# Straight operand stores, interleaved reads of PSUM: one change to a fused transformer kernel

## The chip, the cores and the metric

The kernel runs on one core of one Trainium2 chip. TensorE (PE) does the matrix products, VectorE (DVE), ScalarE (ACT) and GpSimd (POOL) the elementwise work, and SyncE (SP) issues the transfers. The metric is the device time of one launch in microseconds, as the median of several runs.

## The reference

One sequence of 512 tokens and 1024 channels goes through two blocks, in fp32. The first has two layers, each a mixer and a convolutional FFN; the second has two layers, each with four parallel branches, a mixture of experts and a per-layer gate.

```python
def first_block(x, ...):                       # DEPTH = 2
    for layer in range(DEPTH):
        n = rmsnorm(h, norm_g)
        h = h + (rglru_mixer(n, ...) if layer % 2 == 0 else nsa_mixer(n, ...))
        h = h + conv_ffn(rmsnorm(h, ffn_norm_g[layer]), ...)
    return rmsnorm(h, final_norm_g)

def rglru_mixer(x, ...):
    y_br, x_br = jnp.split(x @ w_in, 2, axis=-1)
    xc = causal_dwconv(x_br, conv_w, conv_b)           # 4 taps
    g = sigmoid(blockwise(xc @ gate_w) + gate_b)       # 10 blocks of 128, two gates
    ...                                                # a, bterm from the gates
    h = associative_scan(a, bterm)
    return (h * gelu(y_br)) @ w_out

def conv_ffn(x, ...):
    a, b = jnp.split(x @ w_in, 2, axis=-1)
    return (gelu(causal_dwconv(a, conv_w, conv_b)) * b) @ w_out

def second_block(x, p, ...):
    for i in range(DEPTH):
        h = rms_norm(x, g_mix[i])
        branches = [gqa(h), bidir_ssd(h), diff_attention(h), spatial_gating(h)]   # 256 wide each
        gates = sigmoid(h @ w_branch_gate[i])          # 4 x 1024
        x = x + sum_n(gates_n * (branches_n @ w_branch[i, n])) @ w_out[i]
        x = x + expert_choice_moe(rms_norm(x, g_moe[i]), ...)      # 16 experts, 64 tokens each
        x = x + sigmoid(rms_norm(x, g_ple[i]) @ w_ple_gate[i]) * (p[i] @ w_ple[i])
    return rms_norm(x, g_final)
```

## The kernel before

Activations are kept transposed: channels on the 128 partitions, the 512 tokens along the columns, eight tiles of channels in `hT`. Each fp32 operand is held as two fp32r parts, a high one and the rest, so a product takes three matmuls of 512 columns: high by high, low by high, high by low (`dense`, L443 to L445, and `proj_wide`, L453 to L455). Weights come as a stream of chunks of 512 KB, of which ACT makes the high part (`wh`, L237) and DVE, in some stretches POOL, the low part (`wl`, L238).

Activation operands are made the same way: ACT writes the high part, DVE the rest. `split` (L350, L351) does it for finished rows (xch and xcl of the recurrent blocks, uh and ul, gh and gl in the FFN, oh and ol of the branches, bch and bcl of the state-space branch), `feed` (L360, L361) for the normalised input of a projection (xh, xl), and `mixer_out` (L1264, L1265) for the merged branches.

The matmuls always read the operand through `woven`, that is in the address order 0, 256, 1, 257 and so on. What PSUM then holds depends on how the operand was stored. Most operands are stored through `woven` too: the writer goes through the source in address order and jumps by 256 columns (1024 bytes) at each element, so PSUM's columns come out straight and are read straight. The feeds of the NSA input and of the second block's branches, the NSA's compressed rows and a part of the state-space operands are stored straight; PSUM's columns are then interleaved, and their first reader undoes it with `halves(out), unwoven(ps)`, which writes two halves of 256 columns from a PSUM read with a step of two. The RMS norm's factor is applied behind the product, by that reader (times `RB`).

There is no planner: each engine runs its instructions in the order in which the code issues them. In the recurrent mixer `xfront(i)` (projection, four taps, split) is issued ahead of `xback(i - 1)` (two gates, L519 to L523), then come ten `yblock` (L541 to L548) and the output projection. In the second block `gate_merge` (L1206 to L1216) runs between the pieces of the next branch; behind the last branch its rows end in `mu` (L1215), POOL adds them to `mg`, and `mixer_out` turns `mg` into the operand of the output projection.

Of the kernel before, what the change touches and what calls it, by code (L numbers as in the profile page):

```python
# [11 lines left out]
F32 = mybir.dt.float32  # L12
# [3 lines left out]
OP = mybir.AluOpType  # L16
# [3 lines left out]
P = 128  # L20
# [262 lines left out]
class Kern:  # L283
# [174 lines left out]
    def proj(self, name, idx, col, m=P):  # L458
# [5 lines left out]
        return ps  # L464

    def res_out(self, name, idx, uh, ul, rows, after):
        nc = self.nc
        for d in range(KD):
            ps = self.psum()
            self.dense(ps, [(name, idx, r, d * P) for r in rows], uh, ul)  # L470
            nc.vector.tensor_add(self.hT[:, d, :], ps, self.hT[:, d, :])
            if after:
                after(d)

    def rglru(self, nxt):
        nc = self.nc
        with ExitStack() as es:
# [20 lines left out]
            def xfront(i):  # L498
                ps = self.proj("lru_w_in", 0, LRU + i * P)
                x = xp[i % 2]  # L500
                nc.vector.tensor_mul(x[:, 3:3 + S], ps, self.RB)
                c = two.tile([P, S], F32, name="c")
                nc.scalar.activation(c, x[:, 3:3 + S], AF.Identity, scale=self.p("lru_cw", 3 * LB + i),
                                     bias=self.p("lru_cb", i))
                for j in range(3):
                    nc.vector.scalar_tensor_tensor(c, x[:, j:j + S], self.p("lru_cw", j * LB + i), c,
                                                   op0=OP.mult, op1=OP.add)
                xch = two.tile([P, S], F32R, name="xch")
                xcl = two.tile([P, S], F32R, name="xcl")
# [30 lines left out]
            def yblock(i):  # L540
                ps = self.proj("lru_w_in", 0, i * P)  # L541
                y = two.tile([P, S], F32, name="y")
                nc.vector.tensor_mul(y, ps, self.RB)
                nc.scalar.activation(y, y, AF.Gelu_apprx_tanh)
# [45 lines left out]
    def ffn(self, l, nxt, side=iter(())):  # L590
        nc = self.nc
        HB = FB // 2
        with ExitStack() as es:
# [9 lines left out]
            def pair(f):  # L603
                ps = self.proj("ffn_w_in", l, f * P)
                a = ap[f % 2]
                nc.vector.tensor_mul(a[:, 2:2 + S], ps, self.RB)
                c0 = two.tile([P, S], F32, name="fc0")
# [8 lines left out]
                g = two.tile([P, S], F32, name="g")  # L616
                nc.vector.tensor_mul(g, pb, c0)
                GH.append(ring.tile([P, S], F32R, name="gh"))
# [18 lines left out]
    def nsa(self, nxt):  # L637
        nc = self.nc
        W = "nsa_w_in"
        with ExitStack() as es:  # L640
# [17 lines left out]
            for j in range(2):  # L658
# [13 lines left out]
                CL.append(cp.tile([P, CW], F32R, name=f"cfl{j}"))  # L672
                self.split(CH[j], CL[j], cf, False)

# [106 lines left out]
            def oproj(half, ds, after):  # L781
# [5 lines left out]
                for d in ds:  # L787
                    ps = self.psum()
                    self.dense(ps, [("nsa_w_out", 0, (half * 4 + j) * P, d * P) for j in range(4)], uh, ul)
                    nc.vector.tensor_add(self.hT[:, d, :], ps, self.hT[:, d, :])  # L790
                    if after:
                        after(d)
                    yield
# [118 lines left out]
            def finish(qt, g):  # L912
# [12 lines left out]
                qs = slice(qt * P, (qt + 1) * P)  # L925
                hs = slice(qt * P // 2, (qt + 1) * P // 2)
                uh, ul = woven(uh)[:, :, hs], woven(ul)[:, :, hs]
                nc.scalar.activation(uh, plain(u), AF.Copy)
                nc.vector.tensor_sub(ul, plain(u), uh.bitcast(F32))

# [262 lines left out]
    def gate_merge(self, l, n, o, tp, first):  # L1193
        nc = self.nc
        for d in range(KD):
# [15 lines left out]
            if first:  # L1211
                nc.vector.scalar_tensor_tensor(m, t, 1.0, pb, op0=OP.add, op1=OP.mult)
            else:
                u = tp.tile([P, S], F32, name="mu", tag="mg", bufs=3)
                nc.vector.scalar_tensor_tensor(u, t, 1.0, pb, op0=OP.add, op1=OP.mult)  # L1215
                nc.gpsimd.tensor_add(m, m, u)  # L1216
# [42 lines left out]
    def mixer_out(self, l):  # L1259
        nc = self.nc  # L1260
        for d in range(KD):
            m = self.mg[d // 4][:, d % 4]
            xh, xl = woven(self.xh[:, d]), woven(self.xl[:, d])
            nc.scalar.activation(xh, plain(m), AF.Copy, scale=0.5)  # L1264
            nc.vector.scalar_tensor_tensor(xl, plain(m), 0.5, xh.bitcast(F32), op0=OP.mult, op1=OP.subtract)  # L1265
        lg = self.pso.tile([P, S], F32, name="o")
# [10 lines left out]
        for d in range(KD):  # L1277
            ps = self.psum()
            self.dense(ps, [("w_out_2", l, k * P, d * P) for k in range(KD)], self.xh, self.xl)
            h = self.hT[:, d, :]  # L1280
            nc.vector.tensor_add(h, ps, h)
            rr = self.mo2.tile([P, 2, S], F32R, name="rr", tag="xd")
            rh, rl = woven(rr[:, 0]), woven(rr[:, 1])
            nc.scalar.activation(rh, plain(h), AF.Copy, scale=self.p("g_moe", d))
            nc.vector.scalar_tensor_tensor(rl, plain(h), self.p("g_moe", d), rh.bitcast(F32), op0=OP.mult, op1=OP.subtract)
            R[d] = rh, rl
            self.sqlast = self.feed_sq(d, self.sq)
# [25 lines left out]
        self.lg = self.mo2.tile([NE, S], F32, name="lg", tag="sg")  # L1313
        nc.scalar.activation(self.lg, lg[:NE], AF.Copy)
        self.ple_proj(l, 0, pre[0], (1, 2))
# [116 lines left out]
    def gqa_branch(self, l, o, one, two):  # L1432
# [18 lines left out]
        for t in range(T):  # L1451
# [25 lines left out]
            for j, dst in enumerate((QT, KT)):  # L1477
# [6 lines left out]
                if j:  # L1484
                    out, src = woven(dst)[:, :, t * P // 2:(t + 1) * P // 2], plain(src)
                if j:
                    nc.vector.tensor_copy(out, src)
                else:
                    nc.scalar.activation(out, src, AF.Copy)
        E, PE, PO = {}, {}, {}  # L1490

        def logits(qt, h):
# [8 lines left out]
            den = self.small.tile([P, 1], F32, name="gden")  # L1501
            nc.scalar.activation(e, ps, AF.Exp, scale=-1.0, bias=mn, accum_out=den)
            nc.vector.reciprocal(den, den)
            nc.gpsimd.tensor_scalar(e, e, den, 1.0, op0=OP.mult, op1=OP.mult)

        def values(qt, b):
# [8 lines left out]
            if b:  # L1515
                c = slice(qt * P // 2, (qt + 1) * P // 2)
                oh, ol = woven(o[0])[:, :, c], woven(o[1])[:, :, c]
                v = plain(po[:, :256].rearrange("p (b q) -> p b q", b=2))
                nc.scalar.activation(oh, v, AF.Copy)
                nc.vector.tensor_sub(ol, v, oh.bitcast(F32))  # L1520

# [25 lines left out]
    def ssd_branch(self, l, o, one, two):  # L1547
# [52 lines left out]
        def conv(j):  # L1600
# [16 lines left out]
            r = one.tile([P, S], F32R, name=f"bch{j // 2}"), one.tile([P, S], F32R, name=f"bcl{j // 2}")  # L1617
            self.split(*r, c, j >= 4)
            return r
# [17 lines left out]
        for g in range(2):  # L1637
# [5 lines left out]
            for i in range(T):  # L1643
# [4 lines left out]
                nc.tensor.matmul(pg, bl[:, sl], woven(ch), start=False, stop=True)  # L1648
                nc.scalar.activation(G[:, i], pg, AF.Copy)
            yield 0  # L1650
# [213 lines left out]
    def moe(self, l):  # L1864
        nc = self.nc
        keep, two, three = self.mo1, self.mo2, self.mo3
        if True:
# [181 lines left out]
            def combine(pairs, ds, last):  # L2049
                new = [p for p in pairs if p not in DT]  # L2050
                dts = two.tile([P, 2, S], F32R, name="DT", tag="xd") if new else None
                for i, p in enumerate(new):
# [5 lines left out]
                    DT[p] = dts[:, i]  # L2058
                    nc.vector.tensor_scalar(woven(DT[p]), plain(pb), self.c("slot"), None, op0=OP.is_equal)
                for d in ds:  # L2060
                    ps = self.pst.tile([P, S], F32, name="t")
                    for i, p in enumerate(pairs):
# [3 lines left out]
                                         stop=(i == len(pairs) - 1))  # L2066
                    nc.vector.tensor_add(self.hT[:, d, :], ps, self.hT[:, d, :])
                    if last:
# [30 lines left out]
    def ple_proj(self, l, d, ps, part=None):  # L2099
# [4 lines left out]
        if d % 2 == 0:  # L2104
            self.pbs = self.wraw.tile([P, 2, S], F32, name="pbs", tag="wraw")
        nc.scalar.activation(self.pbs[:, d % 2], ps, AF.Copy)
        if d % 2:
            nc.sync.dma_start(self.pbd[:, d - 1:d + 1], self.pbs)

    def ple(self, l):  # L2110
        nc = self.nc
        with ExitStack() as es:
# [5 lines left out]
            for d in range(KD):  # L2118
                pg = self.proj("w_ple_gate_2", l, d * P)
                t = two.tile([P, S], F32, name="pg")  # L2120
                nc.vector.tensor_mul(t, pg, self.RB)
                nc.scalar.activation(t, t, AF.Tanh, scale=0.5)
# [63 lines left out]
```

## Time and profile before

| | |
|---|---|
| median of 3 runs | 3520.5 us (3515.93 to 3523.99) |
| the profiled execution's own time | 3526.27 us |
| its span | 3524.5 us |
| mean granted TensorE clock | 0.981 |
| PE busy | 3373.1 us, 96% of the span, 16172 matmuls |
| DVE busy | 1778.4 us, 50% |
| ACT busy | 1322.8 us, 38% |
| POOL busy | 471.6 us, 13% |

Busy times are sums over one engine; idle time of an engine other than the bottleneck costs nothing by itself. The granted clock is the share of TensorE's full speed that it was given. Times in the rows further down are microseconds from the span's start unless marked ns.

### The profile page before, as it was taken

What the parts mean: (1) busy time and instruction counts of PE and PEld (TensorE: products, weight loads), DVE (VectorE), ACT (ScalarE), POOL (GpSimd) and SP (SyncE); (2) the same over time, 40 slices, a digit from 0 to 9 for tenths busy, and PEclk for the clock granted to TensorE, in tenths of its full rate; (3) what the DMA queues carried; (4) which work ended last, traced back from release to release, by engine and by line L of the source; (5) the groups of instructions that cost most, each with busy time, mean ns of one, the idle gap of its engine ahead of it and who ended that gap; (6) DMA issues with size and microseconds to landing.
All of it is one profiled execution on the core that took longest, in us unless ns stands there. A gap on an engine that the chain in (4) does not pass through costs nothing.

```text
span 3524.5 us, 42265 instructions
## 1 busy us (share of the span) xinstructions
PE 3373.1 (96%) x16172; PEld 2359.2 (67%) x16172; DVE 1778.4 (50%) x3181; ACT 1322.8 (38%) x2211; POOL 471.6 (13%) x354
## 2 busy tenths in 40 slices
PE   6899999999999999999998999999999998999997
PEld 5778888876678888876887433326876887433325
DVE  7755454467766465766666011116666666111016
ACT  5644233356654244445545101004445545100004
POOL 4221011022121012111012000002111012000002
PEclk9999999899999999999999999999999999999998
DMA  3233332210013333212244999995221245999993
GB/s 112 72 102 133 107 102 102 101 54 30 31 60 102 102 102 119 78 66 66 93 174 163 375 404 419 419 419 196 79 72 64 89 179 177 388 404 419 419 419 124
DMA packets 173491, 629.06 MB, mean 178 GB/s; under 512 B 19557, under 2 KB 20069, under 8 KB 172521
## 3 DMA queue, kind: packets, MB, share of 16 engines
q1 hardware_dynamic: 173288, 626.36, 47.3%
q8 instruction: 127, 2.08, 0.2%
q14 instruction: 76, 0.61, 0.1%
HBM read 618.14 MB, written 8.14 MB: 178 GB/s over the span
## 4 chain that ended last, share of the span: by engine, by line
PE 76%; DVE 11%; DMA 5%; ACT 4%; issue 2%; POOL 1%; DVEq 0%; SPq 0%; ACTq 0%; POOLq 0%
PE mm L444 13%; PE mm L443 13%; PE mm L445 13%; PE mm L1987 10%; PE o L1987 5%; DMA eraw<-in_exw 3%; DVE wl L238 2%; PE o L893 1%; DMA wraw<-in_exw 1%; PE t L877 1%; PE mm L1969 1%; PE o L1657 1%; PE o L1796 1%; DMA raw<-in_exw 1%; PE t L1539 1%
## 5 line engine op out<-in xcount | busy, mean ns | idle before, releaser
L443 PE MATMUL mm<-xh,wh 128*128 128x512 f32 (+1 forms) x1936 | 750.8, 388 | 13.4 <-DVE mu L1215 10.7
L445 PE MATMUL mm<-xh,wl 128*128 128x512 f32 (+1 forms) x1936 | 744.4, 385 | 4.3 <-DVE wl L238 3.7
L444 PE MATMUL mm<-xl,wh 128*128 128x512 f32 (+1 forms) x1936 | 744.3, 384 | 0.0
L238 DVE TENSOR_TENSOR wl<-wraw,wh 128x1024 fp32r<-128x1024 f32 x356 | 449.1, 1262 | 302.5 <-ACT wh L237 297.6
L237 ACT ACTIVATE wh<-wraw 128x1024 fp32r<-128x1024 f32 x378 | 398.5, 1055 | 503.5 <-PE mm L444 331.6
L443 PEld LDWEIGHTS mm<-xh,wh 128*128 128x128 f32 (+1 forms) x1936 | 369.0, 191 | 80.0 <-DVE mu L1215 12.6
L445 PEld LDWEIGHTS mm<-xh,wl 128*128 128x128 f32 (+1 forms) x1936 | 368.4, 190 | 65.4 <-issue 5.8
L444 PEld LDWEIGHTS mm<-xl,wh 128*128 128x128 f32 (+1 forms) x1936 | 368.8, 191 | 59.5 <-issue 8.2
L375 POOL TENSOR_TENSOR sq<-sq,sqt 128x512 f32<-128x512 f32 x63 | 101.7, 1615 | 1235.4 <-ACT sqt L372 1228.3
L1987 PE MATMUL mm<-eraw,xe 128*64 128x512 f32 x1024 | 242.7, 599 | 0.4 <-DMA eraw<-in_exw 0.4
L1993 DVE TENSOR_TENSOR hid<-sg,mm 128x512 f32<-128x512 f32 x32 | 22.0, 687 | 362.0 <-PE mm L1987 362.0
L1987 PE MATMUL mm<-raw,xe 128*64 128x512 f32 x656 | 162.0, 599 | 1.3 <-DMA raw<-in_exw 0.9
L1987 PEld LDWEIGHTS mm<-eraw,xe 128*64 128x64 f32 x1024 | 70.9, 137 | 134.6 <-issue 114.1
L614 POOL TENSOR_TENSOR fc<-fc,RB 128x512 f32<-128x512 f32 x48 | 84.4, 1758 | 546.4 <-ACT fc L613 546.4
L443 PE MATMUL mm<-gh,wh 128*128 128x512 f32 x384 | 145.7, 379 | 0.0
L445 PE MATMUL mm<-gh,wl 128*128 128x512 f32 x384 | 145.7, 379 | 0.0
L444 PE MATMUL mm<-gl,wh 128*128 128x512 f32 x384 | 145.6, 379 | 0.0
L1216 POOL TENSOR_TENSOR mg<-mg,mu 128x512 f32<-128x512 f32 x48 | 69.9, 1456 | 565.8 <-DVE mu L1215 520.6
L1987 PE MATMUL o<-eraw,hidT 128*64 128x512 f32 x560 | 137.2, 606 | 4.0 <-DMA eraw<-in_exw 3.1
L2041 ACT ACTIVATE yh<-o,af 128x512 fp32r<-128x512 f32 x32 | 22.0, 687 | 295.6 <-PE o L1987 295.6
L1992 ACT ACTIVATE sg<-mm 128x512 f32<-128x512 f32 x32 | 19.1, 597 | 288.8 <-PE mm L1987 288.6
L2042 DVE SCALAR_TENSOR_TENSOR yl<-o,af,yh 128x512 fp32r<-128x512 f32 x32 | 24.0, 751 | 198.5 <-ACT yh L2041 198.3
(524 smaller groups left out, 5883.0 us busy)
## 6 DMA issues: line engine op xcount, KB each, us to landing
eraw<-in_exw SPq DMA_DIRECT2D x396, 512.0 KB, 9.9
wraw<-in_wst SPq DMA_DIRECT2D x378, 512.0 KB, 3.3
raw<-in_exw SPq DMA_DIRECT2D x234, 512.0 KB, 9.9
wraw<-in_exw SPq DMA_DIRECT2D x136, 512.0 KB, 9.9
pbd<-pbs SPq DMA_DIRECT2D x8, 512.0 KB, 4.8
pb<-pbd SPq DMA_DIRECT2D x4, 1024.0 KB, 11.7
tb<-t5d SPq DMA_DIRECT2D x8, 448.0 KB, 3.3
mixt<-in_mix SPq DMA_DIRECT2D x2, 1344.0 KB, 6.4
```

Source lines behind the costliest of these rows:

```text
L237: kb.nc.scalar.activation(h, raw, AF.Copy)
L238: (kb.nc.gpsimd if self.pool else kb.nc.vector).tensor_sub(l, raw, h.bitcast(F32))
L375: nc.gpsimd.tensor_add(acc, acc, t)
L443: nc.tensor.matmul(out, a, h, start=(k == 0), stop=False)
L444: nc.tensor.matmul(out, a, l, start=False, stop=False)
L445: nc.tensor.matmul(out, b, h, start=False, stop=(k == n - 1))
L614: nc.gpsimd.tensor_mul(c0, c0, self.RB)
L877: nc.tensor.transpose(pt[:, r * P:(r + 1) * P], srcs(i, r), self.ident)
L893: nc.tensor.matmul(o[0][c % 2 * HD:(c % 2 + 1) * HD], lhs(i), pe, start=(c < 2), stop=False)
L1216: nc.gpsimd.tensor_add(m, m, u)
L1539: nc.tensor.transpose(pt[:, kb * P:(kb + 1) * P], e[:, kb * P:(kb + 1) * P], self.ident)
L1987: nc.tensor.matmul(ps[e * CAP:(e + 1) * CAP], x[:, k, off + e * CAP:off + (e + 1) * CAP], raw[:, e], start=(k == 0), stop=(k == KD - 1))
```

## The change

Every operand is stored straight: `split`, `feed`, `mixer_out` and the single writers (attention rows, keys, the router's rows, the experts' scatter matrix) lose `woven` and `plain`. The matmuls and their `woven` read stay. So all PSUM columns now come interleaved, and each first reader that was straight gets `halves` on its output and SBUF inputs and `unwoven` on PSUM. A helper, `add_rows`, does so for the sums into `hT`. The count, order and size of the instructions on each engine stay the same. The diff is cut to one place of each kind:

```diff
-    def split(self, h, l, src, weave=True):
-        if weave:
-            h, l, src = woven(h), woven(l), plain(src)
+    def split(self, h, l, src):
         self.nc.scalar.activation(h, src, AF.Copy)
         self.nc.vector.tensor_sub(l, src, h.bitcast(F32))
 
     def feed(self, k, g, sq=True):
         nc = self.nc
         h = self.hT[:, k, :]
-        xh, xl, x = self.xh[:, k], self.xl[:, k], h
-        if isinstance(g, str) and g not in ("nsa_g", "g_mix", "g_next"):
-            xh, xl, x = woven(xh), woven(xl), plain(h)
+        xh, xl = self.xh[:, k], self.xl[:, k]
         g = self.p(g, k) if isinstance(g, str) else g[:, k:k + 1]
-        nc.scalar.activation(xh, x, AF.Copy, scale=g)
-        nc.vector.scalar_tensor_tensor(xl, x, g, xh.bitcast(F32), op0=OP.mult, op1=OP.subtract)
+        nc.scalar.activation(xh, h, AF.Copy, scale=g)
+        nc.vector.scalar_tensor_tensor(xl, h, g, xh.bitcast(F32), op0=OP.mult, op1=OP.subtract)
...
+    def add_rows(self, d, ps):
+        h = halves(self.hT[:, d])
+        self.nc.vector.tensor_add(h, unwoven(ps), h)
...
             def xfront(i):
-                nc.vector.tensor_mul(x[:, 3:3 + S], ps, self.RB)
+                nc.vector.tensor_mul(halves(x[:, 3:3 + S]), unwoven(ps), halves(self.RB))
...
             def xback(i):
-                    nc.scalar.activation(g, pg, AF.Tanh, scale=0.5, bias=gbh[:, j * LB + i:j * LB + i + 1])
+                    nc.scalar.activation(halves(g), unwoven(pg), AF.Tanh, scale=0.5, bias=gbh[:, j * LB + i:j * LB + i + 1])
...
     def mixer_out(self, l):
-            xh, xl = woven(self.xh[:, d]), woven(self.xl[:, d])
-            nc.scalar.activation(xh, plain(m), AF.Copy, scale=0.5)
-            nc.vector.scalar_tensor_tensor(xl, plain(m), 0.5, xh.bitcast(F32), op0=OP.mult, op1=OP.subtract)
+            xh, xl = self.xh[:, d], self.xl[:, d]
+            nc.scalar.activation(xh, m, AF.Copy, scale=0.5)
+            nc.vector.scalar_tensor_tensor(xl, m, 0.5, xh.bitcast(F32), op0=OP.mult, op1=OP.subtract)
...
-            nc.scalar.activation(e, ps, AF.Exp, scale=-1.0, bias=mn, accum_out=den)
+            nc.scalar.activation(halves(e), unwoven(ps), AF.Exp, scale=-1.0, bias=mn, accum_out=den)
```

The other PSUM readers changed like `xfront`'s are the rows of `yblock`, of the FFN (L606, L617), of `mu` (L1215), of the per-layer gate, and the sums into `hT` of `res_out`, the NSA output, `mixer_out` and the experts. On ACT, like `xback`'s: the softmax of the branch attention (L1502, 32 times), the state-space scores (L1649, 16), the router's logits (L1314, 2) and the per-layer rows (L2106, 16).

## Rows read from the trace of the kernel before

**Rows 1.** The page: busy us (share of the span) and instructions of each engine.

```profile
PE 3373.1 (96%) x16172; PEld 2359.2 (67%) x16172; DVE 1778.4 (50%) x3181; ACT 1322.8 (38%) x2211; POOL 471.6 (13%) x354
```

**Rows 2.** PE's waits, whole span: releaser: us in total, times, longest us.

```profile
PE s L519 <- ACT xch L350: 16.1, 9, 4.0
...
PE mm L443 <- DVE mu L1215: 10.7, 4, 5.1
PE mm L454 <- DVE xl L361: 9.7, 12, 2.3
...
PE s L1646 <- ACT bch L350: 4.4, 4, 1.6
```

**Rows 3.** Windows: us, busy us (instructions) of each engine, granted clock, DMA share, GB/s.

```profile
17.00:28.00 11.00, 5.62 (x23) 3.66 (x22) 11.00 (x9) 5.26 (x7) 9.22 (x5) 1.00 0.29 95
28.00:49.00 21.00, 16.39 (x67) 13.44 (x65) 15.84 (x49) 5.41 (x7) 7.44 (x4) 0.84 0.22 76
49.00:144.00 95.00, 74.79 (x302) 59.12 (x303) 84.09 (x89) 66.83 (x80) 35.23 (x19) 0.95 0.18 61
1022.00:1029.00 7.00, 7.00 (x23) 5.60 (x23) 3.54 (x13) 0.06 (x1) 0.50 (x1) 0.55 0.21 75
1862.00:1869.00 7.00, 6.81 (x18) 5.53 (x19) 2.35 (x3) 1.98 (x3) 2.11 (x1) 0.57 0.69 239
2916.00:2920.00 4.00, 4.00 (x11) 3.24 (x12) 1.70 (x2) 1.21 (x2) 2.05 (x1) 0.58 0.47 157
```

**Rows 4.** Lines, 194 to 243 us: busy us, mean ns | idle before, releasers.

```profile
L360 ACT ACTIVATE xh<-hT,prmt 128x512 fp32r<-128x512 f32 x8 | 9.7, 1212 | 14.7 <-DVE hT L471 12.3 <-DVE ap L601 2.4
...
L361 DVE SCALAR_TENSOR_TENSOR xl<-hT,prmt,xh 128x512 fp32r<-128x512 f32 x8 | 9.4, 1169 | 7.6 <-ACT xh L360 7.6
```

**Rows 5.** Lines, 571 to 628 us.

```profile
L361 DVE SCALAR_TENSOR_TENSOR xl<-hT,prmt,xh 128x512 fp32r<-128x512 f32 x8 | 6.0, 749 | 2.4 <-ACT xh L360 2.4
L360 ACT ACTIVATE xh<-hT,prmt 128x512 fp32r<-128x512 f32 x8 | 5.7, 714 | 9.7 <-DVE hT L471 9.7
```

**Rows 6.** Lines, 1586 to 1588.2 us.

```profile
L351 DVE TENSOR_TENSOR bcl<-cv,bch 128x512 fp32r<-128x512 f32 x1 | 0.7, 680 | 0.0
L350 ACT ACTIVATE bch<-cv 128x512 fp32r<-128x512 f32 x1 | 0.6, 637 | 1.0 <-DVE cv L1616 1.0
```

**Rows 7.** Lines of DVE, whole span.

```profile
L1206 DVE TENSOR_TENSOR mg<-mm,RB 128x512 f32<-128x512 f32 x64 | 44.3, 691 | 33.6 <-PE mm L445 33.5
...
L606 DVE TENSOR_TENSOR ap<-mm,RB 128x512 f32<-128x512 f32 x48 | 33.2, 691 | 21.7 <-PE mm L445 17.7 <-ACT RB L422 4.0
```

**Rows 8.** Lines of ACT, whole span.

```profile
L1502 ACT ACTIVATE e<-s,gmn 128x512 f32<-128x512 f32 x32 | 21.8, 683 | 16.5 <-DVE gmn L1499 14.9 <-DVE gden L1503 1.7
...
L523 ACT ACTIVATE gt<-s,gbh 128x512 f32<-128x512 f32 x20 | 12.8, 679 | 6.4 <-PE s L521 6.3
```

**Rows 9.** PE's waits, 0 to 30 us.

```profile
PE mm L454 <- DVE xl L361: 5.4, 4, 2.3
```

**Rows 10.** Lines of DVE, 8.5 to 28 us.

```profile
L361 DVE SCALAR_TENSOR_TENSOR xl<-hT,prmt,xh 128x512 fp32r<-128x512 f32 x8 | 13.8, 1779 | 0.3 <-ACT xh L360 0.3
```

**Rows 11.** DVE's timeline, 178 to 186 us: start us, us, instruction, idle before.

```profile
178.94 1.12 DVE L351 TENSOR_TENSOR ul<-y,uh 128x512 fp32r<-128x512 f32 x1 [3.25 <-ACT uh L350]
179.91 1.21 DVE L238 TENSOR_TENSOR wl<-wraw,wh 128x1024 fp32r<-128x1024 f32 x1
...
184.94 1.10 DVE L351 TENSOR_TENSOR ul<-y,uh 128x512 fp32r<-128x512 f32 x1 [3.23 <-ACT uh L350]
```

**Rows 12.** ACT's timeline, 177 to 181 us.

```profile
177.79 1.12 ACT L350 ACTIVATE uh<-y 128x512 fp32r<-128x512 f32 x1 [1.38 <-POOL y L545]
178.71 1.05 ACT L237 ACTIVATE wh<-wraw 128x1024 fp32r<-128x1024 f32 x1
```

**Rows 13.** DVE's timeline, 1851 to 1862.5 us.

```profile
1854.86 4.29 DVE L1265 SCALAR_TENSOR_TENSOR xl<-mg,xh 128x512 fp32r<-128x512 f32 x4
...
1861.15 0.99 DVE L1215 SCALAR_TENSOR_TENSOR mu<-mg,mm 128x512 f32<-128x512 f32 x1
```

More of the change, by code (lines that the diff above doesn't have):

```diff
@@ L470, in res_out @@
             self.dense(ps, [(name, idx, r, d * P) for r in rows], uh, ul)
-            nc.vector.tensor_add(self.hT[:, d, :], ps, self.hT[:, d, :])
+            self.add_rows(d, ps)
             if after:
@@ L542, in yblock @@
                 y = two.tile([P, S], F32, name="y")
-                nc.vector.tensor_mul(y, ps, self.RB)
+                nc.vector.tensor_mul(halves(y), unwoven(ps), halves(self.RB))
                 nc.scalar.activation(y, y, AF.Gelu_apprx_tanh)
@@ L605, in pair @@
                 a = ap[f % 2]
-                nc.vector.tensor_mul(a[:, 2:2 + S], ps, self.RB)
+                nc.vector.tensor_mul(halves(a[:, 2:2 + S]), unwoven(ps), halves(self.RB))
                 c0 = two.tile([P, S], F32, name="fc0")
@@ L616, in pair @@
                 g = two.tile([P, S], F32, name="g")
-                nc.vector.tensor_mul(g, pb, c0)
+                nc.vector.tensor_mul(halves(g), unwoven(pb), halves(c0))
                 GH.append(ring.tile([P, S], F32R, name="gh"))
@@ L672, in nsa @@
                 CL.append(cp.tile([P, CW], F32R, name=f"cfl{j}"))
-                self.split(CH[j], CL[j], cf, False)
+                self.split(CH[j], CL[j], cf)
             pv = [self.mm.tile([P, S], F32, name="mm") for _ in range(2)] + \
@@ L789, in oproj @@
                     self.dense(ps, [("nsa_w_out", 0, (half * 4 + j) * P, d * P) for j in range(4)], uh, ul)
-                    nc.vector.tensor_add(self.hT[:, d, :], ps, self.hT[:, d, :])
+                    self.add_rows(d, ps)
                     if after:
@@ L925, in finish @@
                 qs = slice(qt * P, (qt + 1) * P)
[L926 to L929, printed above, removed]
+                self.split(uh[:, :, qs], ul[:, :, qs], u)
             def spread(a, b):
@@ L1211, in gate_merge @@
             if first:
-                nc.vector.scalar_tensor_tensor(m, t, 1.0, pb, op0=OP.add, op1=OP.mult)
+                nc.vector.scalar_tensor_tensor(halves(m), halves(t), 1.0, unwoven(pb), op0=OP.add, op1=OP.mult)
             else:
                 u = tp.tile([P, S], F32, name="mu", tag="mg", bufs=3)
-                nc.vector.scalar_tensor_tensor(u, t, 1.0, pb, op0=OP.add, op1=OP.mult)
+                nc.vector.scalar_tensor_tensor(halves(u), halves(t), 1.0, unwoven(pb), op0=OP.add, op1=OP.mult)
                 nc.gpsimd.tensor_add(m, m, u)
@@ L1280, in mixer_out @@
             h = self.hT[:, d, :]
-            nc.vector.tensor_add(h, ps, h)
+            self.add_rows(d, ps)
             rr = self.mo2.tile([P, 2, S], F32R, name="rr", tag="xd")
[L1283 to L1286, printed above, removed]
+            rh, rl = rr[:, 0], rr[:, 1]
+            nc.scalar.activation(rh, h, AF.Copy, scale=self.p("g_moe", d))
+            nc.vector.scalar_tensor_tensor(rl, h, self.p("g_moe", d), rh.bitcast(F32), op0=OP.mult, op1=OP.subtract)
+            R[d] = woven(rh), woven(rl)
             self.sqlast = self.feed_sq(d, self.sq)
@@ L1313, in mixer_out @@
         self.lg = self.mo2.tile([NE, S], F32, name="lg", tag="sg")
-        nc.scalar.activation(self.lg, lg[:NE], AF.Copy)
+        nc.scalar.activation(halves(self.lg), unwoven(lg[:NE]), AF.Copy)
         self.ple_proj(l, 0, pre[0], (1, 2))
@@ L1484, in gqa_branch @@
                 if j:
-                    out, src = woven(dst)[:, :, t * P // 2:(t + 1) * P // 2], plain(src)
-                if j:
                     nc.vector.tensor_copy(out, src)
@@ L1515, in values @@
             if b:
[L1516 to L1520, printed above, removed]
+                c = slice(qt * P, (qt + 1) * P)
+                self.split(o[0][:, :, c], o[1][:, :, c], po[:, :256].rearrange("p (b q) -> p b q", b=2))
         steps = [(qt, h) for qt in range(T) for h in range(4)]
@@ L1617, in conv @@
             r = one.tile([P, S], F32R, name=f"bch{j // 2}"), one.tile([P, S], F32R, name=f"bcl{j // 2}")
-            self.split(*r, c, j >= 4)
+            self.split(*r, c)
             return r
@@ L1648, in ssd_branch @@
                 nc.tensor.matmul(pg, bl[:, sl], woven(ch), start=False, stop=True)
-                nc.scalar.activation(G[:, i], pg, AF.Copy)
+                nc.scalar.activation(halves(G[:, i]), unwoven(pg), AF.Copy)
             yield 0
@@ L2058, in combine @@
                     DT[p] = dts[:, i]
-                    nc.vector.tensor_scalar(woven(DT[p]), plain(pb), self.c("slot"), None, op0=OP.is_equal)
+                    nc.vector.tensor_scalar(DT[p], pb, self.c("slot"), None, op0=OP.is_equal)
                 for d in ds:
@@ L2066, in combine @@
                                          stop=(i == len(pairs) - 1))
-                    nc.vector.tensor_add(self.hT[:, d, :], ps, self.hT[:, d, :])
+                    self.add_rows(d, ps)
                     if last:
@@ L2105, in ple_proj @@
             self.pbs = self.wraw.tile([P, 2, S], F32, name="pbs", tag="wraw")
-        nc.scalar.activation(self.pbs[:, d % 2], ps, AF.Copy)
+        nc.scalar.activation(halves(self.pbs[:, d % 2]), unwoven(ps), AF.Copy)
         if d % 2:
@@ L2120, in ple @@
                 t = two.tile([P, S], F32, name="pg")
-                nc.vector.tensor_mul(t, pg, self.RB)
+                nc.vector.tensor_mul(halves(t), unwoven(pg), halves(self.RB))
                 nc.scalar.activation(t, t, AF.Tanh, scale=0.5)
```

## The prediction

> **What bounds the kernel now.** I read the page's busy times first: TensorE (PE) is busy for 3373.1 of 3524.5 us, 96% [rows 1]. The change leaves its stream of matmuls as it is, and DVE and ACT matter only where PE waits for them. So the whole prize is PE's idle time, about 151 us, and what its lower clock costs behind a wait. Next the waits of PE by releaser [rows 2]: among the longest the reader is to see three that write operands, namely the conv split of the recurrent block (xch, 16.1 us in 9 waits), the feeds (xl, 9.7 us in 12) and the B/C split of the state-space branch (bch, 4.4 us in 4). A fourth, mu (10.7 us in 4), writes no operand, but seven operand stores stand ahead of it on DVE. The windows come last: what DVE and POOL do in those stretches, and where the granted clock falls to 0.55 to 0.58 behind a wait [rows 3]. In the FFN and the experts PE waits for almost nothing, so the 48 gated splits that get shorter there count as nothing; PE's matmuls cover them.
>
> **What a straight store is worth.** One line has both kinds. The feed in woven order takes 1169 ns on DVE and 1212 on ACT [rows 4]; the same lines in straight order take 749 and 714 [rows 5], so 0.42 and 0.50 us less. The split takes 1.12 us woven on both engines [rows 11, 12] and, straight, 637 ns on ACT and 680 on DVE [rows 6]: 0.48 and 0.44 less. I use these for all stores of 512 columns; I assume that the shapes of 2 x 256 or 2 x 2 x 64 gain the same.
>
> **What the step of two costs.** The reader of PSUM now steps by two fp32. On DVE the kernel before already does that in the gate product: 691 ns over 64 of them, against 691 for the FFN's straight read over 48 [rows 7]. I take 0. For ACT the trace has no such read: 86 instructions get one, 20 in the recurrent gates and 32 in the softmax (679 and 683 ns [rows 8]), the other 34 copies. Bounds: nothing, as on DVE, or what a jumping store costs ACT, 0.48 us. I take 0, since of the two rows only DVE's reads PSUM; a gain is excluded, as the read was straight.
> [...]
>
> **The sum.** Nothing moves: each engine gets the same instructions in the same order, so each term is a shorter wait.
> (a) First feed, up to 28 us. PE waits 5.4 us in 4 waits for xl [rows 9]; DVE is busy all of 17 to 28 us and POOL 9.2 of 11 [rows 3]. The eight xl take 1779 ns on average there [rows 10], more than the 1169 with a quieter POOL. If DVE sets the pace, 8 x 0.42 = 3.4; with a little from the first xh, 3.5. Bounds 2 (POOL sets half of it) to 5 (nearly all of the waits).
> [...]
> (b) Recurrent blocks, 49 to 144 us. Each block goes xp, c, three taps, xch, xcl, with PE waiting for xch nine times. DVE is busy 84.1 of 95 us [rows 3]. Nine waits at 0.48 give 4.3; DVE's own relief of ten xcl at 0.44 adds part of another 4.4. I take 6, bounds 4 to 9.
> (c) Gated blocks, 144 to 191 us. The loop is y (DVE), gelu (ACT), product (POOL), uh (ACT), ul, wl (DVE), next y; one turn is 6.0 us, from ul at 178.94 to ul at 184.94 [rows 11], where PE, with a matmul every 0.209 us on the whole kernel's average [rows 1], needs 5.0 for its 24. uh falls by 0.48. ul starts that much earlier and is itself 0.44 shorter, but wl then waits for wh, which follows uh on ACT and ends at 179.76 now, 179.28 then: wl starts at about 179.3 in place of 179.91 [rows 11, 12]. One turn is about 0.57 shorter, still over 5.0. Five such turns, two before them at about 0.75, a pair of ul in the first (0.86) and the last uh (0.48) give 5.7. Bounds 3 (PE or the weights take over) to 8.
> (d) Merged rows into the output projection, in both layers. Before mu stand seven xl, a wl and the gate's product on DVE; four of the xl take 4.29 us in a row [rows 13]. PE needs the sum that mu goes into, and waits 10.7 us for it in all, 5.1 the longest [rows 2]. xl waits for xh, so ACT would set the pace if its xh fell less. Seven at 0.45 are 3.2; I take 3.6 for the first layer, where the stores are slowest, and 3.0 for the second, together 6.6. Bounds 5 to 7.
> (e) The other feeds at the start of a projection: before the second FFN and, twice, before the per-layer gate. Of xl's 9.7 us 5.4 are in (a), so 4.3 lie here in eight waits [rows 2, 9], and PE waits about 1 us more for an xh in each, 7.3 together. hT, xh and xl follow one another there, so each turn loses 0.9. I take two thirds, 4.8, bounds 3 to 6.5.
> (f) bch, four waits [rows 2]: 4 x 0.45 = 1.8, bounds 1 to 2.5.
> (g) Eight more places with one shorter store each ahead of PE (branch outputs, keys of both layers, the router's rows, attention rows): 8 x 0.45 = 3.6. Some of these waits are shorter than that, so bounds 1.5 to 5.
> (h) Clock. [...] I count all 7.8, bounds 0 to 8.
> Sum: 3.5 + 6 + 5.7 + 6.6 + 4.8 + 1.8 + 3.6 + 7.8 = 39.8. The low ends give 19.5, the high ends 51. The profiled execution took 3526.3 us (its span and 1.8 around it), so 3486.5 for one like it. The median of the runs is 5.8 below that; from it, 3520.5 - 39.8 = 3480.7, so 3481 us.
>
> **Rivals.**
> 1. The waits fill up again. Behind each shorter store the next link is late: POOL's product, POOL beside DVE in (a), wh behind xh on ACT, or the weights. For it: in (c) a third of the gain is lost to wh already. Against it: in (d) and (e) little else is queued. Then only about half of (a) to (g), 32 in all, comes, and little of the clock: 10 to 30 less, at 18 some 3502 us.
> 2. The clock gives more. At a granted clock of 0.84 from 28 to 49 us and 0.95 from 49 to 144 [rows 3], 21 x 0.16 + 95 x 0.05 = 8 us are lost there of which I counted none. With them 48 less: 3473 us, and 3461 with the high ends of the other terms too. Against it: the longest wait for xch is 4.0 us, and 0.9 of it goes.
> 3. ACT reads PSUM slowly at a step of two. 86 reads become dearer by p each. The recurrent gates and the softmax lie in loops where PE waits, the other copies mostly don't; were all 86 exposed, the loss would be 86 p, equal to the gain at p = 0.46 us. Only above that is the kernel slower; at 0.85 (two and a quarter times as long) 73 are lost, 33 net: 3554 us. At 0.48 with half of it exposed 19 are left: 3501. For it: no ACT row. Against it: DVE's rows show nothing at all.
> That the change doesn't shorten the stores is hardly open, with both kinds of the same line in the trace.
>
> **How the numbers follow.** My forecast of 30 to 45 less gets 0.55, rival 1 0.25, rival 2 0.13, rival 3 with a slower kernel 0.03; 0.04 are left for gains under 7 us. The likeliest case's own range is 3476 to 3491. To leave out no more than 2 in 10 it has to take in most of rivals 1 and 2: from 3463 to 3502, near the low ends of the sum (3501). A measurement of this kernel can tell about 0.2%, 7 us, from no change: faster 0.93, within it 0.04, slower 0.03.
>
> **What would show it.** In the profile after: feeds at about 0.75, splits at 0.64 to 0.68; the reads at 0.69 on DVE and 0.68 on ACT; waits for xch near 11 us, for mu near 4, the turn of (c) at 5.45; no half clock behind (d). Gates of 0.9 us or more on ACT would bear out rival 3; wh or POOL as the new releaser, or DVE's stores still at 1.1 beside POOL, rival 1. The forecast is wrong if the waits for xch and mu don't fall, or if they fall and PE's idle time doesn't.

## The result, and the profile after

The changed kernel takes 3483.8 us, the median of 4 runs (3483.68 to 3484.64), against 3522.24 for the kernel before, the median of 4 (3515.93 to 3524.86). The ratio is 0.9894, with a 95% interval of 0.9877 to 0.9911. The forecast was 3481 in a range of 3463 to 3502, so the sum came out; its parts did not all do so.

The waits of PE in the profile after, whole span, with the same columns as [rows 2]:

```profile
PE s L519 <- ACT xch L348: 12.6, 6, 3.6
...
PE mm L450 <- DVE xl L357: 6.1, 8, 1.9
PE mm L439 <- DVE mu L1212: 5.7, 4, 2.7
...
PE s L1638 <- ACT bch L348: 2.3, 2, 1.2
```

Each of the four releasers is down, xch from 16.1 to 12.6 us, mu from 10.7 to 5.7, xl from 9.7 to 6.1 and bch from 4.4 to 2.3. The lines of DVE over the whole span (busy us, mean ns, then idle time and its releasers) show what shortened them and what didn't:

```profile
L1203 DVE TENSOR_TENSOR mg<-mm,RB 128x512 f32<-128x512 f32 x64 | 43.9, 686 | 35.1 <-PE mm L441 35.1
...
L349 DVE TENSOR_TENSOR gl<-g,gh 128x512 fp32r<-128x512 f32 x48 | 33.2, 692 | 32.1 <-ACT gh L348 32.0
L606 DVE TENSOR_TENSOR ap<-mm,RB 128x512 f32<-128x512 f32 x48 | 33.2, 692 | 23.5 <-PE mm L441 19.4 <-ACT RB L418 4.0
...
L357 DVE SCALAR_TENSOR_TENSOR xl<-hT,prmt,xh 128x512 fp32r<-128x512 f32 x32 | 32.7, 1033 | 9.5 <-ACT xh L356 9.5
...
L357 DVE SCALAR_TENSOR_TENSOR xl<-hT,layt,xh 128x512 fp32r<-128x512 f32 x24 | 25.1, 1059 | 3.3 <-ACT xh L356 3.3
```

The low parts of the split are at 692 ns where a woven one took 1.12 us [rows 11], and L606, which now reads PSUM with a step of two, is at 692 where the straight read took 691 [rows 7]. The xl didn't get to 749: they still take 1.03 to 1.06 us. The lines of ACT answer to [rows 8]:

```profile
L348 ACT ACTIVATE gh<-g 128x512 fp32r<-128x512 f32 x48 | 30.2, 629 | 123.7 <-DVE g L617 123.7
...
L1497 ACT ACTIVATE e<-s,gmn 128x512 f32<-128x512 f32 x32 | 21.9, 686 | 15.7 <-DVE gmn L1494 14.0 <-DVE gden L1498 1.7
...
L523 ACT ACTIVATE gt<-s,gbh 128x512 f32<-128x512 f32 x20 | 12.7, 680 | 6.5 <-PE s L521 6.5
...
L1641 ACT ACTIVATE G<-s 128x512 f32<-128x512 f32 x16 | 9.1, 597 | 14.1 <-PE s L1640 13.9
```

The gates took 679 ns with a straight read and take 680 with a step of two, the softmax 683 and 686, the state-space scores (L1641) 596 and 597. ACT pays nothing either.

What the difference is made of shows best when the start of the same matmul is compared in the two profiled executions, since PE's stream is the same in both (times are those of the kernel before; the executions took 3526.3 and 3483.7 us, so some 4 us more apart than the medians):

| stretch, us | forecast | measured |
|---|---|---|
| 0 to 28, (a) | 3.5 | 3.7 |
| 49 to 144, (b) | 6.0 | 6.4 |
| 144 to 192, (c) | 5.7 | 3.9 |
| 677 to 718, the NSA's compress stage | 0 | 14.1 |
| the three feeds of (e), and their clock | 4.8 + 3.1 | 2.0 - 0.9 - 1.0 |
| 1852 to 1870 and 2906 to 2921, (d), and its clock | 6.6 + 4.7 | 3.7 + 2.5 |
| 1560 to 1700 and 2527 to 2869, (f) among them | 1.8 | 2.5 + 1.3 |
| all the rest, (g) among it | 3.6 | 4.8 |

Not all of this is the stores. Of the 3.7 us of the first row 1.1 stand ahead of the first matmul, whose start lies anywhere from 7.2 to 8.6 us in the kept traces, whichever the stores. Low stretches of the clock that came or went are in several rows: of the 3.8 in the row of (f), 1.7 are one at 1564 us that only the kernel before has, and the products behind the four bch start 0.5, 0.4, 0.5 and 0.4 us earlier, 1.8 in all.

The largest part is one that the forecast didn't have. Windows over that stage, of the kernel before and then of the changed one (us, busy us of each engine, granted clock, DMA share, GB/s):

```profile
676.80:717.70 40.90, 40.90 (x199) 40.26 (x198) 11.14 (x15) 10.39 (x15) 0.00 (x0) 0.50 0.30 103
```

```profile
661.10:688.40 27.30, 26.98 (x202) 26.36 (x201) 10.90 (x15) 10.52 (x15) 0.00 (x0) 1.00 0.44 144
```

The matmuls are the same, some 200 in each window. Before, TensorE was granted its lower level (0.50 in the window) for all of it but the first 2.2 us; after, the higher (1.00). Ahead of it PE has waited in both for the same thing, 0.9 us for the gates' rows; this line stands in the waits of both:

```profile
PE mm L699 <- DVE kk L696: 0.9, 1, 0.9
```

What is operand and what is PSUM reader in this stage was not touched by the change.

### The profile page after: what moved, and what is told of

Read it like the earlier page. It is cut to its first block, busy times and chain, and to the rows that moved or that the text cites. A ratio compares the mean times of both kernels' runs of the same rounds, so it can differ in the third digit from the quotient of the medians.

```text
span 3481.6 us, 42254 instructions
## 1 busy us (share of the span) xinstructions
PE 3352.9 (96%) x16172; PEld 2343.5 (67%) x16172; DVE 1717.9 (49%) x3181; ACT 1255.6 (36%) x2211; POOL 460.0 (13%) x354
## 4 chain that ended last, share of the span: by engine, by line
PE 77%; DVE 10%; DMA 7%; ACT 3%; issue 2%; POOL 1%; DVEq 0%; SPq 0%; ACTq 0%; POOLq 0%
PE mm L439 14%; PE mm L440 14%; PE mm L441 13%; PE mm L1979 11%; PE o L1979 4%; DMA eraw<-in_exw 3%; DMA raw<-in_exw 2%; DVE wl L238 2%; PE o L893 2%; PE t L877 1%; PE mm L1961 1%; PE o L1649 1%; PE o L1788 1%; ACT wh L237 1%; DMA wraw<-in_exw 1%
## 5 line engine op out<-in xcount | busy, mean ns | idle before, releaser
L371 POOL TENSOR_TENSOR sq<-sq,sqt 128x512 f32<-128x512 f32 x63 | 88.9, 1412 | 1240.4 <-ACT sqt L368 1233.2
```

Of the source, the lines that this page charges most:

```text
L371: nc.gpsimd.tensor_add(acc, acc, t)
```

## The experiments

**1 to 3. Does the moment decide?** Extra matmuls, put where the granted clock is 1.00 in both kernels and one matmul follows the other by 0.21 to 0.22 us, move the stage in time and change nothing else.

```diff
             nc.tensor.matmul(out, a, h, start=(k == 0), stop=False)     # in dense; ahead of it:
+            for _ in range(self.extra if k == 0 else 0):
+                nc.tensor.matmul(out, a, h, start=True, stop=True)
```

with `extra` set for one projection some 40 us ahead of the stage: 13 or 16 in the kernel before, 3 in the changed one.

> The kernel before with 13 extra matmuls (the first one of a projection repeated) some 30 us ahead of the NSA's compress stage, so that the stage and the pause of about 1 us ahead of it come 2.8 us later; nothing else differs. Theory 1 (the moment): in the kernel before the clock fell at the start of that stage because of the moment at which the pause came, not because of the stores. Then the stage runs at a granted clock of about 1.00 instead of 0.50 over 41 us, which saves 14, and the whole takes some 11 us less than before, about 3510. Theory 2 (the stores): the straight stores kept the clock up in the kernel after. Then the stage stays at half clock and the whole takes 2.8 us more than before, about 3525.

> The same with 16 extra matmuls, a shift of 3.4 us. [...] A third reading, that extra matmuls as such keep the clock up: full clock, 11 us less.

> The changed kernel with 3 extra matmuls at the same place, a shift of 0.65 us, which puts the pause where it stood in the kernel before against the low stretches. Theory 1: the compress stage falls to half clock over about 41 us, and the whole takes 14 + 0.65 us more, about 3498. Theory 2: the stage stays at full clock, 0.65 us more, about 3484.5.

The 3.41 us of theory 1 is what the clock's records of the two profiled executions show: low stretches start at 31.67, 86.28, 106.76, 130.65 and 188.68 us of the kernel before and at 27.05, 78.25, 105.56 and 173.83 of the changed one, and all sixteen of each lie whole multiples of 3.413 us apart.

The third came out as theory 1 has it: 3498.45 us (7 executions, 3494.3 to 3499.6), 14.6 over the changed kernel, and the stage at the lower level:

```profile
662.90:703.80 40.90, 40.90 (x198) 40.26 (x198) 11.31 (x15) 10.29 (x15) 0.00 (x0) 0.50 0.32 103
```

The other two gave no single answer, and showed why. With 13 extra matmuls five of ten executions took 3506 to 3513 us at a mean granted clock of 0.985 to 0.988, and five 3524 to 3531 at 0.979 to 0.980. With 16, two of ten took 3507 to 3509, the others 3522.6 to 3533. The kernel before itself, run beside all experiments, does both: 52 of 58 executions at 0.978 to 0.983, six at 0.985 to 0.987 and 3503.5 to 3510 us. Only one execution of each kernel is profiled; in the others the level in this stage is inferred from the mean clock and from a time that is some 12 to 20 us longer. So the level in this stage isn't fixed by the kernel but a matter of odds. The odds of staying at the higher level are one in ten for the kernel before, and a shift of the stage alone moves them: to five in ten at 2.8 us, and for the changed kernel to none of seven at 0.65 us. Two in ten with 16 can't be told from the kernel before. Theory 2, that the straight stores keep the clock up, is out, and so is the third reading, that extra matmuls do. Theory 1 holds only as odds, and what the moment has to be measured against isn't shown: in the two profiled executions of the changed kernel, both at the higher level here, the stage begins at 659.1 and 660.1 us, which is further apart than the shift of the third experiment.

**4 and 8. The pause.** The transposes of the NSA's gates are moved behind the compress stage, in the kernel before and in the changed one.

```diff
-            pt = self.psum()                      # ahead of the compress stage
-            for t in range(T):
-                nc.tensor.transpose(pt[:, t * 48:(t + 1) * 48], gc[:, t * P:(t + 1) * P], ...)
-            ...
             for j in range(2):                    # compress stage
...
+            pt = self.psum()                      # the same lines, behind it
```

> The kernel before with the four transposes of the NSA gates moved behind the compress stage, so that PE doesn't wait for their rows ahead of it (0.9 us less idle there). If the pause is what brings the clock down, the stage runs at full clock: 14 to 15 us less than before, about 3507. If the stage's own short matmuls (160 columns) bring it down whatever stands ahead, half clock stays and the time is 1 us less at most.

> The changed kernel with the gates' transposes moved behind the compress stage: a version that might beat both. About 1 us of waiting goes ahead of the stage, and the clock there is at its full level already: 3482 to 3483, unless later low stretches move by it (1.7 us for each that comes or goes).

Without the pause the kernel before takes 3504.5 us (10 executions, 3502.8 to 3508.4), and all ten are at a clock of 0.986 to 0.988. With the same short matmuls and no wait ahead of them, no execution fell. In the profiled execution the whole stage is at the higher level:

```profile
671.20:697.50 26.30, 26.30 (x192) 26.27 (x191) 9.62 (x12) 9.56 (x11) 0.00 (x0) 1.00 0.45 154
```

That the wait as such is what brings the clock down isn't shown by this: without it and the transposes the stage also starts sooner, 0.2 us behind the last matmul of the projection ahead of it instead of 1.6, and a shift of 0.65 us was enough to move the odds.

The changed kernel without the pause takes 3481.4 us (4 executions, 3475.2 to 3485.0). These two, with the stage at the higher level on both sides, are the fairest pair in the study: the stores and reads are worth 23.1 us. Low stretches elsewhere are still in it, and differ by execution: by the clock's records the lower level cost 44.0 us in the profiled execution of the first and 50.6 in that of the second, and 44.1 in that of its repetition below, which is 22.0 us shorter than the first.

**9 and 10. Odds of the changed kernel, and the version without the pause again.**

> The changed kernel once more, in more executions. If the compress stage's clock is a matter of the moment, so that the kernel before falls in nine of ten executions and this one mostly doesn't, then a few of these executions should come some 14 us above 3484, at a mean granted clock of 0.981 instead of 0.987. If the straight stores keep the clock up, none does.

> The changed kernel with the gates' transposes behind the compress stage, again, beside the changed kernel on one chip: does the version beat it? Without the pause no execution should fall to half clock in that stage. 1 us less than the changed kernel if its clock stays up, 3481 to 3483; several us less on the average if that one falls in some executions.

One of the six executions of the changed kernel took 3496.2 us at 0.982, the others 3479.0 to 3484.4. With the four runs of the result that is one in ten at the low level, so theory 2 is out here too. The version without the pause took 3481.5 (3474.9 to 3483.9); over both of its experiments nine executions, none low. Whether it beats the changed kernel's good executions by its 2 us these runs don't settle, nor whether it falls more rarely: none of nine against one of ten is no difference yet.

**5 and 6. Whose stores?** `woven` and `plain` put back into the changed kernel on one engine's stores alone (in `split` for rows of 512 columns, in `feed` and in `mixer_out`).

```diff
-        self.nc.vector.tensor_sub(l, src, h.bitcast(F32))                      # e5, DVE
+        self.nc.vector.tensor_sub(woven(l), plain(src), woven(h).bitcast(F32))
-        self.nc.scalar.activation(h, src, AF.Copy)                             # e6, ACT
+        self.nc.scalar.activation(woven(h), plain(src), AF.Copy)
```

> The changed kernel with DVE's stores of 512 columns (the low parts in feed, split and the merged rows) in woven order again, ACT's straight; the operands' columns are then not in one order, only the times mean something. In the FFN, where PE covers them, the low part is made with a jumping read and a straight store in even rows and a straight read and a jumping store in odd ones. Theory A: DVE sets the pace of the recurrent blocks (88% busy), so most of the 6.4 us gained from 49 to 144 us before goes again, as do the 2.5 gained at each merged output, but less than half of the 3.9 in the gated blocks (the chain there goes over uh and wh on ACT). Theory B: ACT's stores are on the path: less than a third goes in the recurrent blocks. In the FFN: if the store is what costs, odd rows take 1.1 us and even ones 0.69; if the read is, the other way round; if either, both 1.1.

> The other half: ACT's stores of 512 columns (the high parts) in woven order again, DVE's straight; again only the times mean something. Theory A: in the recurrent blocks less than half of the 6.4 us goes, in the gated blocks most of the 3.9 (uh and wh behind it are 0.48 later each turn, so a turn of 6.0 instead of 5.6). Theory B: most goes in both. At the merged output xl waits for xh, so about 2 of 2.5 us go in each layer.

By matmul starts against the changed kernel:

| stretch | gained by the change | lost again, DVE woven | lost again, ACT woven |
|---|---|---|---|
| first feed | 3.7 | 2.7 | 0.4 |
| recurrent blocks | 6.4 | 3.5 | 1.2 |
| gated blocks | 3.9 | 2.0 | 2.4 |
| merged output, PE's wait for mu alone, first layer / second | 2.5 / 2.5 | 2.4 / 2.4 | 0.6 / 0.9 |

Theory A holds for the recurrent blocks, where DVE has more than half and ACT a fifth, and for the gated blocks, where ACT has the larger share, though DVE's is half and not less. At the merged output I expected 2 us from ACT in each layer and PE waited 0.6 and 0.9 longer. PE's waits there, DVE woven and then ACT woven, against 5.7 us in four for the changed kernel:

```profile
PE mm L446 <- DVE mu L1219: 10.6, 4, 5.1
```

```profile
PE mm L442 <- DVE mu L1215: 7.2, 4, 3.2
```

With ACT woven, the first layer's xl wait for xh 0.9 us in all instead of 0.2, the second's 1.4 instead of 0.5; for the rest DVE's seven stores set the pace. As a whole DVE woven takes 3503.2 us in the five of eight executions whose mean clock is 0.985 or 0.986, 19.4 more; ACT woven is at 3492 to 3497 in the three of eight at 0.986 or 0.987, 8 to 13 more. The other three (3522.8 to 3525.9) and five (3498.0 to 3505.7) have a lower mean clock; ACT woven's profiled execution is one of them and is low in the compress stage. (In both, the feeds that were straight before are woven too.) In the FFN of the first of them, the first line has the jumping store, the second the jumping read:

```profile
L354 DVE TENSOR_TENSOR gl<-g,gh 128x512 fp32r<-128x512 f32 x24 | 26.4, 1100 | 16.7 <-ACT gh L348 16.7
...
L352 DVE TENSOR_TENSOR gl<-g,gh 128x512 fp32r<-128x512 f32 x24 | 17.0, 708 | 15.5 <-ACT gh L348 15.3
```

1100 against 708 ns, with 692 for straight on both sides: the store costs, the read (of one of the two inputs) hardly does.

**7 and 11. What holds the xl at 1.05 us?**

```diff
-        nc.gpsimd.tensor_add(acc, acc, t)      # in feed_sq; left out in e7
+        nc.vector.tensor_add(acc, acc, t)      # e11, on top of the version without the pause
```

> The changed kernel without POOL's additions to the sum of squares in the feeds (the norm's factor is then wrong, which changes no time). Theory P: the xl that still take 1.03 to 1.06 us on average are held up by POOL's sums beside them; without these all of them take 0.75, and at the feeds ahead of the per-layer gate and the second FFN PE waits for xl about 1 us less in each. Rival: they wait for something else (ACT's high part, PSUM), and stay above 1 us.

> The same, with the feeds' additions to the sum of squares on DVE instead of POOL. Leaving them out altogether saved 22 us. If it is POOL's hold on DVE's second operand that cost them, an addition on DVE of 0.7 us is cheaper than the 0.3 to 1 us that each xl and its neighbours are held, where the additions stand beside them, and costs nothing in the FFNs, where DVE waits for PE: 4 to 10 us less than without it, 3472 to 3478. Rival: DVE sets the pace of these feeds, so that eight additions of 0.7 us are added where eight holds of 0.3 to 1 go: the same within 3 us.

With the additions left out, the kernel takes 3461.7 us (3459.8 and 3463.7), 22 less. About half of that is the clock: what the lower level cost by its records went from 45.7 to 35.4 us. The rest shows in PE's waits, of the changed kernel and then without the additions:

```profile
PE t L396 <- POOL sq L425: 4.6, 5, 2.8
```

```profile
PE mm L449 <- DVE xl L357: 2.5, 2, 1.3
PE t L395 <- POOL sq L424: 1.9, 4, 0.6
```

The waits for xl fell from 6.1 us in eight to 2.5 in two, both at the first feed, so that none is left at the others. PE's waits for POOL's last sum itself, the sum of squares that it turns into the norm, fell by 2.7 us; that part doesn't go through DVE. The xl with the layers' own parameters, those ahead of the per-layer gates among them, go from 1059 to 776 ns on average:

```profile
L357 DVE SCALAR_TENSOR_TENSOR xl<-hT,prmt,xh 128x512 fp32r<-128x512 f32 x32 | 28.7, 909 | 9.5 <-ACT xh L356 9.5
...
L357 DVE SCALAR_TENSOR_TENSOR xl<-hT,layt,xh 128x512 fp32r<-128x512 f32 x24 | 18.3, 776 | 3.4 <-ACT xh L356 3.4
```

Not all xl come to 0.75 us, as theory P had it: the eight of the first feed, where other sums stay on POOL, take 1.39 on average. What they waited for can be seen in the changed kernel itself, ahead of the first layer's gate. The timeline of POOL, then that of DVE (start us, us, instruction, idle before):

```profile
2365.36 3.13 POOL L371 TENSOR_TENSOR sq<-sq,sqt 128x512 f32<-128x512 f32 x2 [6.72 <-ACT sqt L368]
```

```profile
2365.59 3.45 DVE L357 SCALAR_TENSOR_TENSOR xl<-hT,layt,xh 128x512 fp32r<-128x512 f32 x2
...
2370.43 0.75 DVE L357 SCALAR_TENSOR_TENSOR xl<-hT,layt,xh 128x512 fp32r<-128x512 f32 x1 [0.19 <-ACT xh L356]
```

While POOL adds two squares, two xl take 3.45 us; behind it one takes 0.75. Of the 24 xl with the layers' own parameters, the ten with a sum of POOL beside them for half their time or more take 1.16 to 1.77 us, the seven with none 0.74 to 0.75. Both inputs of an xl are in SBUF; L2113, the gates' row, has one of its two in PSUM, and eight of its 16 instructions, with POOL's sums of squares beside them as long, take 0.68 to 0.69 us, as do those without. With the sums on DVE the kernel takes 3471.9 us (5 executions, 3467.5 to 3472.4), at the edge of what was expected, at a ratio of 0.9861 to the kernel before (0.9842 to 0.988). That beats both, the changed kernel by 11.8 us with no execution of the one within the other's. Against the version without the pause it is 9.6 us less, within the 4 to 10 expected. Of that 6.9 us come from 750 to 1000 us, at the feed behind the NSA output and ahead of it, but 5.1 of these are lower-level time that this execution doesn't have there; 2.6 and 4.0 come at the two per-layer gates, 1.7 of the 4.0 again from the clock. In the FFNs the added sums cost nothing.

## Why the prediction came out

**The steps that held.** The straight splits took what the straight rows had shown (692 and 629 ns, against 680 and 637), and the step of two costs nothing on either engine, so rival 3 is out. (a), (b) and (f) came within their bounds, (f) at its forecast by the starts behind bch alone.

**(c) Right mechanism, too large.** The turn went from 6.0 to 5.61 us instead of 5.45. The changed kernel's timelines of DVE and ACT for one turn:

```profile
159.68 0.69 DVE L349 TENSOR_TENSOR ul<-y,uh 128x512 fp32r<-128x512 f32 x1 [2.83 <-ACT uh L348]
160.62 1.23 DVE L238 TENSOR_TENSOR wl<-wraw,wh 128x1024 fp32r<-128x1024 f32 x1 [0.25 <-ACT wh L237]
...
165.29 0.69 DVE L349 TENSOR_TENSOR ul<-y,uh 128x512 fp32r<-128x512 f32 x1 [2.84 <-ACT uh L348]
```

```profile
159.01 0.63 ACT L348 ACTIVATE uh<-y 128x512 fp32r<-128x512 f32 x1 [1.45 <-POOL y L545]
159.55 1.04 ACT L237 ACTIVATE wh<-wraw 128x1024 fp32r<-128x1024 f32 x1
```

wl starts 0.03 us behind wh's end, as foreseen, and 1.61 behind uh's start where it was 2.12 [rows 11, 12]: 0.51 of the 0.57. But the turn fell by only 0.39, so 0.12 was lost again, more than half of it around POOL's product, for which ACT now waits 1.45 instead of 1.38 us.

**(d) The wait was misread.** I had PE waiting for the sum that POOL makes of mu. The seven xl, of the kernel before and then of the changed one, with what stands between them there, and then POOL's two sums of the changed kernel:

```profile
1852.43 1.44 DVE L1265 SCALAR_TENSOR_TENSOR xl<-mg,xh 128x512 fp32r<-128x512 f32 x1 [0.97 <-ACT xh L1264]
...
1859.26 2.36 DVE L1265 SCALAR_TENSOR_TENSOR xl<-mg,xh 128x512 fp32r<-128x512 f32 x2
```

```profile
1817.56 1.79 DVE L1262 SCALAR_TENSOR_TENSOR xl<-mg,xh 128x512 fp32r<-128x512 f32 x1 [0.19 <-ACT xh L1261]
...
1820.41 2.48 DVE L1262 SCALAR_TENSOR_TENSOR xl<-mg,xh 128x512 fp32r<-128x512 f32 x4
1822.82 0.68 DVE L1203 TENSOR_TENSOR mg<-mm,RB 128x512 f32<-128x512 f32 x1
1823.42 1.28 DVE L1262 SCALAR_TENSOR_TENSOR xl<-mg,xh 128x512 fp32r<-128x512 f32 x2
1824.62 0.67 DVE L1212 SCALAR_TENSOR_TENSOR mu<-mg,mm 128x512 f32<-128x512 f32 x1
```

```profile
1817.52 1.28 POOL L1213 TENSOR_TENSOR mg<-mg,mu 128x512 f32<-128x512 f32 x1 [4.79 <-DVE mu L1212]
1825.44 2.12 POOL L1213 TENSOR_TENSOR mg<-mg,mu 128x512 f32<-128x512 f32 x1 [6.63 <-DVE mu L1212]
```

PE's first matmul behind its wait, before and after:

```profile
1862.19 0.79 PE L443 MATMUL mm<-xh,wh 128*128 128x512 f32 x1 [5.14 <-DVE mu L1215]
```

```profile
1825.35 0.48 PE L439 MATMUL mm<-xh,wh 128*128 128x512 f32 x1 [2.66 <-DVE mu L1212]
```

PE goes on at 1825.35 (last line), just behind mu and ahead of POOL's sum, which starts at 1825.44. No matmul reads mu, so what PE waits for must be mu's reading of PSUM. The seven xl took 1.44 + 4.29 [rows 13] + 2.36 = 8.1 us and take 1.79 + 2.48 + 1.28 = 5.6, so 2.5 less, and the wait fell by just that, from 5.14 to 2.66. My 3.6 came from seven times the full difference; but the first of them starts with a sum on POOL (1817.52 to 1818.80) and became longer, not shorter. These lines also correct the section on the kernel before, which says that the engines run in the order in which the code issues: the code issues mg and mu of the last tile ahead of the xl, and the built program puts seven xl ahead of mu, five of them ahead of mg.

**(e) and (a): POOL's hold.** This was rival 1's mechanism and I gave it too little. Two xl took 3.45 us beside POOL's sums and one 0.75 without, while L2113, with an input in PSUM, stayed at 0.68 to 0.69 beside them; by what means POOL holds the xl up no run shows. For (a), where I weighed it, it took little: a pair of xl beside POOL's sums went from 4.14 to 3.45 us there. For (e), where I didn't, it mattered: PE's waits for xl there shrank only from 4.3 us in eight waits to 3.5 in six, and without POOL's additions all six go. Ahead of its low stretch each per-layer gate had gained 0.7 us.

**(h) The step that failed.** I took it, from a clock of 0.95 beside waits of 1.8 us in the recurrent blocks [rows 2, 3], that a shorter wait gives the clock back. The 7.8 is an estimate from the granted clock of [rows 3], 7 x 0.43 + 4 x 0.42 + 7 x 0.45 us; that all of it comes back with shorter waits no run shows. It did in part: behind the feed of the second FFN and in the first layer's (d) the low stretches are shorter; in the second layer's nothing changed, 1.7 us lost in both. But new ones came, at both per-layer gates among other places. Windows of the changed kernel, at the second FFN's feed, the two merged outputs and the first per-layer gate; the first three answer to the last three of [rows 3]:

```profile
991.00:998.00 7.00, 6.32 (x24) 5.19 (x25) 3.65 (x14) 1.23 (x2) 1.27 (x1) 0.76 0.24 75
1824.00:1831.00 7.00, 5.65 (x18) 4.68 (x19) 3.12 (x5) 2.00 (x4) 2.12 (x1) 0.76 0.78 263
2873.00:2880.00 7.00, 7.00 (x26) 5.83 (x26) 1.83 (x3) 2.20 (x4) 1.95 (x1) 0.76 0.79 288
2375.00:2379.00 4.00, 4.00 (x13) 3.23 (x13) 3.60 (x11) 0.00 (x0) 0.00 (x0) 0.57 0.28 90
```

Added up over the whole span, without the compress stage and the last 20 us, TensorE stood at its lower level for 71.7 us before and 71.7 after. Between these two executions (h) was 0, not 7.8. It isn't fixed either: in the other profiled execution of the changed kernel (3479.0 us) the sum is 58.0, which is 6.8 us of time less, and the low stretches at the per-layer gates aren't there. Of the nine executions at the higher level in the compress stage eight took 3483.5 to 3484.6 us, so 0 is the common case.

**The total was right by two errors that cancel.** My terms without (h) were 32.0, and the pause-free pair gives 23.1 for them; (h) added 7.8 that didn't come; and the compress stage gave about 14 that I hadn't counted, because I looked for the clock only behind waits that the change shortens, and PE is busy all through that stage. So it was luck that the total fitted. Against like executions the change is worth 21 to 27 us: at the high level the kernel before has 3505.2 (median of six) and the changed one 3483.7 (nine), at the low level 3522.7 (52) and 3496.2 (one) or 3497.8 (the third experiment less its shift). In the medians it shows as 38.4 because the kernel before falls in nine executions of ten and the changed one in one of ten.

What stays open is what sets those odds, and why executions of one program differ. The runs show that the moment of the stage matters, and that no execution fell where the pause ahead of it was gone, 24 in three kernels (10, 9 and the 5 with the sums on DVE); whether it is the wait or the moment that matters there they don't separate.

## What to carry to other kernels

Put the stride on the side that is free: here a jumping store cost 0.4 to 0.5 us for 512 columns, a jumping SBUF read 0.02 and a PSUM read with a step of two nothing. Price a shorter instruction by what runs beside it, too: the xl, with two SBUF inputs, came down to 1.03 and 1.06 us on average beside POOL's sums, and not to the 0.75 of a straight store alone. And before a gain is put down to a change, look for a stretch in which the clock's level differs between the two profiles and ask whether the change touched it; repeat the kernel before often enough to see whether it has two levels of its own.

## What the runs showed that I had not expected

A stage of short matmuls stayed at the lower level for 41 us although PE was busy all through, at a cost of 14 us; by the mean clock it did so in 52 of 58 executions of the kernel before. A shift of 0.65 us brought the same about in the changed kernel in seven executions of seven. And POOL's sums of squares cost 22 us of the changed kernel, though all of POOL has but 1% of the chain on its page: about half through the clock, and the rest through PE's waits for xl and for the sums themselves.
